# Squares and scaling of the first projection moved into the second one, and a second queue for the first input block

## The chip, the cores and the metric

The kernel runs on one core of a Trainium2 chip. The metric is the time of one execution on the device in microseconds (us). A core has engines with a queue of instructions each, which run beside one another and wait for each other by semaphores: TensorE (PE; its weight loads are PEld in the profile), VectorE (DVE), ScalarE (ACT), GpSimd (POOL) and SyncE (SP), which here only issues transfers.

## The reference

Two layers on x, 256 tokens by 2048 columns, in float32: an even one (retention and compressed, selected and windowed attention) and an odd one (convolution and dilated attention). Each normalizes its input and multiplies it by one wide weight matrix. The part around the change, cut:

```python
def rms_norm(x, gain):
    y = x * lax.rsqrt(jnp.mean(x * x, axis=-1, keepdims=True) + NORM_EPS)
    return y * gain
...
def compress(t, pos_emb, w1, w2):          # t: (batch, head, token, 128)
    idx = np.arange(n_cmp)[:, None] * CMP_STRIDE + np.arange(CMP_LEN)[None, :]
    blk = (t[:, :, idx] + pos_emb).reshape(B, G, n_cmp, CMP_LEN * d)
    return jax.nn.gelu(blk @ w1) @ w2
...
h = rms_norm(x, norm_g) @ w_in
rq, rk, rv, rz, nq, kc, vc, ks, vs, kw, vw, ng, nz = split_cols(h, EVEN_SPLITS)
kcmp = rms_norm(compress(heads(kc, G), pos_k, k_w1, k_w2), k_g[0])
vcmp = compress(heads(vc, G), pos_v, v_w1, v_w2)
```

Since the sum over a token's 2048 squares gives one factor per token, the kernel multiplies by the gain ahead of the matmul and by the token's factor `rstd` behind it.

## The kernel before

The kernel multiplies in slices of 512 weight columns, "projections". `project` goes through 2048 rows in four chunks of 512 rows (1 MB each, tile `raw`, three buffers). Of each chunk ACT makes the rounded part `wh` (L103) and DVE the rest `wl` (L104), in halves, and of the input block `xT` (four k-tiles of 128 rows by 256 tokens, held transposed) ACT makes `xh` (L185) and DVE `xl` (L186), both times the gain `evn`. PE adds up three products, wh by xh, wl by xh and wh by xl (L139 to L141): 24 matmuls of 512 columns a chunk, 96 a projection, into two PSUM banks `mm` for the two halves of the tokens. There are three such banks, so the next projection's first half can start in the third, and its second half needs the one that the first eviction of the projection before has emptied. Evictions are done by ACT.

The first projection makes `hkv` (keys and values for the compression), the second and the third `hs` (keys and values for the two attentions). In the first one ACT also squares each block of `xT` (L195), DVE sums the squares over k-tiles (L196) and over blocks (L201), PE over partitions with a column of ones (L204), and DVE and POOL make `rstd` from it (L210, L212), which the evictions of `hkv` and of every later projection take (L253). `hkv` is then transposed to `tT` (L274, L304), overlapping windows of it plus a position term are `blk` (L313), split in parts by ACT (L319) and DVE (L320) into `bhl` ahead of the compression's matmuls `cmph` (L340), which run between those of the third projection. `hs` is normed by head (square L260, sum `kn0ss` L262, POOL L168 and L169, product L265) and then transposed by PE.

Far later a row `rrow`, `rstd` along the free axis (`token_row`, L222 to L226), is made for the rotary tables in `pb` (L580, L581) and other projections.

Instructions are put in order by a scheduler of the framework with its own model of times; `tc.high_priority` puts an instruction ahead. The order on each engine is then fixed. All transfers go through SP's queue in the order that it gives them.

## Time and profile before

| | |
|---|---|
| time, median of 3 runs | 966.43 us (966.43, 966.43, 968.01) |
| profiled execution, its own time | 967.98 us |
| its span | 966.2 us |
| busy: PE, DVE, ACT, POOL | 950.3 (98%), 649.0 (67%), 521.1 (54%), 146.1 (15%) us |
| mean granted clock of PE | 0.998 |
| transfers | 171.53 MB, mean 178 GB/s |

The profiled execution's time is 1.8 us over its span; parts of a sum that is made from its rows belong to it and not to the median. A time behind "idle before" in a row is how long the engine stood still ahead of it, and behind the arrow stands what released it.

### The profile page before, as it was taken

The numbers are of one execution on the slowest core, as the hardware profiler recorded it, in microseconds if no ns is written. First come the engines' busy times: TensorE is split into PE (matmuls) and PEld (weight loads), VectorE is DVE, ScalarE is ACT, GpSimd is POOL, SyncE is SP. The second block draws the span as 40 slices with busy tenths as digits, with TensorE's granted clock in tenths as the row PEclk, the third lists the DMA queues.
The fourth block names the chain that finished last, engine by engine and source line by source line (L and its number), as shares of the span: only waits on it lengthen the run. The fifth ranks groups of instructions, "written<-read, shape, count | busy, mean of one in ns | idle before, by whom it ended". The sixth has DMA issues, their size and how long they took to land.

```text
span 966.2 us, 15609 instructions
## 1 busy us (share of the span) xinstructions
PE 950.3 (98%) x6401; PEld 873.3 (90%) x6401; DVE 649.0 (67%) x909; ACT 521.1 (54%) x727; POOL 146.1 (15%) x134
## 2 busy tenths in 40 slices
PE   8899999999999999999999999999999999999998
PEld 7688989899998998899999999888768889999998
DVE  7776556965654565655575579899889856545643
ACT  8366645755454444543364475555765556655532
POOL 0111010320211010000000294111771202000000
PEclk9999999999999999999999999999999999999999
DMA  9565753335445454555554445555445544433561
GB/s 314 205 214 181 234 208 132 128 135 175 163 163 185 165 174 175 184 181 197 180 176 174 175 165 185 192 200 175 173 137 214 181 171 171 169 125 144 197 211 73
DMA packets 31944, 171.53 MB, mean 178 GB/s; under 512 B 3328, under 2 KB 9600, under 8 KB 12800
## 3 DMA queue, kind: packets, MB, share of 16 engines
q1 hardware_dynamic: 31872, 170.53, 50.9%
q8 instruction: 50, 0.82, 0.3%
q14 instruction: 22, 0.18, 0.1%
HBM read 168.42 MB, written 2.10 MB: 176 GB/s over the span
## 4 chain that ended last, share of the span: by engine, by line
PE 88%; POOL 4%; ACT 3%; DVE 3%; issue 1%; DMA 0%; SPq 0%; POOLq 0%; ACTq 0%
PE mm L134 14%; PE mm L133 14%; PE mm L135 14%; PE mm L140 12%; PE mm L141 12%; PE mm L139 12%; POOL acc L737 3%; ACT wh L103 1%; PE tr L274 1%; DVE wl L104 1%; PE dpo L864 1%; PE dsc L844 1%; PE cmph L340 1%; DMA raw<-in_ew 0%; PE tr L529 0%
## 5 line engine op out<-in xcount | busy, mean ns | idle before, releaser
L104 DVE TENSOR_TENSOR wl<-raw,wh 128x1024 fp32r<-128x1024 f32 (+2 forms) x326 | 392.8, 1208 | 247.1 <-ACT wh L103 244.8
L103 ACT CAST wh<-raw 128x1024 fp32r<-128x1024 f32 (+2 forms) x326 | 328.8, 1012 | 338.9 <-PE mm L135 177.8
L134 PE MATMUL mm<-xh,wl 128*128 128x256 f32 x1280 | 362.3, 284 | 0.9 <-DVE wl L104 0.9
L133 PE MATMUL mm<-xh,wh 128*128 128x256 f32 x1280 | 360.6, 285 | 2.1 <-ACT wh L103 1.8
L135 PE MATMUL mm<-xl,wh 128*128 128x256 f32 x1280 | 360.4, 284 | 0.0
L134 PEld LDWEIGHTS mm<-xh,wl 128*128 128x128 f32 x1280 | 245.4, 192 | 1.8 <-DVE wl L104 1.5
L133 PEld LDWEIGHTS mm<-xh,wh 128*128 128x128 f32 x1280 | 243.6, 192 | 2.9 <-ACT wh L103 2.3
L135 PEld LDWEIGHTS mm<-xl,wh 128*128 128x128 f32 x1280 | 244.7, 192 | 0.1
L140 PE MATMUL mm<-wl,xh 128*128 128x512 f32 (+1 forms) x608 | 234.5, 387 | 6.1 <-DVE wl L104 6.0
L141 PE MATMUL mm<-wh,xl 128*128 128x512 f32 (+1 forms) x608 | 231.1, 381 | 0.0
L139 PE MATMUL mm<-wh,xh 128*128 128x512 f32 (+1 forms) x608 | 215.3, 384 | 1.4 <-ACT xh L185 0.8
L140 PEld LDWEIGHTS mm<-wl,xh 128*128 128x128 f32 x608 | 115.2, 190 | 31.5 <-DVE wl L104 10.6
L139 PEld LDWEIGHTS mm<-wh,xh 128*128 128x128 f32 x608 | 113.8, 189 | 23.3 <-ACT xh L185 1.1
L141 PEld LDWEIGHTS mm<-wh,xl 128*128 128x128 f32 x608 | 115.0, 189 | 20.7
L727 DVE SCALAR_TENSOR_TENSOR cps<-apad,pb,cps 128x256 f32<-128x256 f32 x180 | 87.5, 486 | 3.5
L737 POOL TENSOR_TENSOR acc<-acc,tap 128x256 f32<-128x256 f32 x60 | 60.1, 1001 | 14.0 <-ACT acc L733 8.4
L736 ACT ACTIVATE tap<-apad,pb 128x256 f32<-128x256 f32 x60 | 28.4, 503 | 16.9 <-POOL acc L737 14.0
L212 POOL TENSOR_TENSOR rstd<-rstd2m,mhalf 128x2 f32<-128x2 f32 x1 | 0.7, 695 | 162.3 <-DVE rstd2m L210 162.3
L593 POOL TENSOR_TENSOR rot<-rot,pb 128x512 f32<-128x512 f32 x8 | 11.1, 1402 | 79.7 <-ACT rot L591 79.6
L517 ACT ACTIVATE p<-p,nm 128x128 f32<-128x128 f32 (+1 forms) x32 | 14.2, 446 | 10.7 <-DVE nm L513 10.6
L196 DVE TENSOR_REDUCE sqs<-sqb 128x256 f32<-128x1024 f32 x8 | 16.0, 2004 | 0.3 <-ACT sqb L195 0.3
L686 DVE TENSOR_TENSOR xT<-mm,xT 128x512 f32<-128x512 f32 (+1 forms) x18 | 11.1, 630 | 5.1 <-PE mm L135 5.1
(272 smaller groups left out, 658.7 us busy)
## 6 DMA issues: line engine op xcount, KB each, us to landing
raw<-in_ow SPq DMA_DIRECT2D x64, 1024.0 KB, 4.8
raw<-in_ew SPq DMA_DIRECT2D x53, 1024.0 KB, 4.9
raw<-in_ewo SPq DMA_DIRECT2D x16, 1024.0 KB, 4.8
raw<-in_owo SPq DMA_DIRECT2D x12, 1024.0 KB, 4.9
raw<-in_ewn SPq DMA_DIRECT2D x8, 536.0 KB, 4.0
raw<-in_ew SPq DMA_DIRECT2D x12, 256.0 KB, 4.7
raw<-in_w1k SPq DMA_DIRECT2D x2, 1024.0 KB, 5.6
raw<-in_w1v SPq DMA_DIRECT2D x2, 1024.0 KB, 4.8
```

The source lines that it names most:

```text
L103: nc.scalar.copy(wh[:, k, :n], r)
L104: nc.vector.tensor_sub(wl[:, k, :n], r, wh[:, k, :n].bitcast(F32))
L133: nc.tensor.matmul(o, wh[:, k, cs], xh[:, kk, :], start=first and j == 0, stop=False, **kw)
L134: nc.tensor.matmul(o, wl[:, k, cs], xh[:, kk, :], start=False, stop=False, **kw)
L135: nc.tensor.matmul(o, wh[:, k, cs], xl[:, kk, :], start=False, stop=last, **kw)
L139: nc.tensor.matmul(o, xh[:, kk, ts], wh[:, k, :n], start=first, stop=False)
L140: nc.tensor.matmul(o, xh[:, kk, ts], wl[:, k, :n], start=False, stop=False)
L141: nc.tensor.matmul(o, xl[:, kk, ts], wh[:, k, :n], start=False, stop=last)
L196: nc.vector.reduce_sum(sqs[0][:, b, :], sq.rearrange("p k s -> p s k"), axis=AX.X)
L727: nc.vector.scalar_tensor_tensor(p, src[:, k:k + S], w[:, k:k + 1], p, op0=ALU.mult, op1=ALU.add)
L736: nc.scalar.activation(tap, src[:, k:k + S], AF.Copy, scale=w[:, k:k + 1])
L737: nc.gpsimd.tensor_add(dst, dst, tap)
```

## The change

The warm-up of PE gets 40 matmuls in place of 36. The first block of `xT` and the gains are loaded by ScalarE's queue and the weights alone by SP's at first. The first k-tile's `xh` is made by DVE. The squares leave the first projection: x is loaded a second time, by tokens (`xtok`, four pieces of 128 tokens by 1024 columns), and ACT squares and sums a piece in one instruction, after the first chunk of the second projection; `rstd` and `rrow` are made from that. The evictions of `hkv` are plain copies, and its transpose is scaled by `rrow`. The windows are made after the third chunk of the second projection in the program's text. The second layer's sum of squares is made by additions.

```diff
-WARM = 36
+WARM = 40
...
-            nc.scalar.activation(xh[:, k, :], x, AF.Copy, scale=g)
+            if first and k == 0:
+                nc.vector.tensor_scalar(xh[:, k, :], x, g, None, op0=ALU.mult)
+            else:
+                nc.scalar.activation(xh[:, k, :], x, AF.Copy, scale=g)
...
         nc.scalar.activation(sq, xT[:, 4 * b:4 * b + 4, :], AF.Square)
-        nc.vector.reduce_sum(sqs[0][:, b, :], sq.rearrange("p k s -> p s k"), axis=AX.X)
+        nc.vector.tensor_add(sq[:, 0:2, :], sq[:, 0:2, :], sq[:, 2:4, :])
+        if b == 0:
+            nc.vector.tensor_add(sqs[0], sq[:, 0, :], sq[:, 1, :])
+        else:
+            nc.vector.tensor_add(sq[:, 0, :], sq[:, 0, :], sq[:, 1, :])
+            nc.vector.tensor_add(sqs[0], sqs[0], sq[:, 0, :])
...
+    with tc.high_priority(offset=4 * HPO):
+        nc.scalar.dma_start(xT[:, 0, :], a["xT"][:, 0, :])
+        nc.scalar.dma_start(evn, a["ev_norm"])
+        nc.scalar.dma_start(xT[:, 1:4, :], a["xT"][:, 1:4, :])
...
-    def first_block(c):
-        load_block(c)
-        if c == 3:
-            for b in range(4):
-                square_block(b)
-            rstd.append(token_rstd(token_squares(sqs[0]), "rstd1"))
-
-    project(ew[0], 512, lhs, evac_to(hkv), lazy=first_block, cut=load_rest)
+    project(ew[0], 512, lhs, lambda t, p: nc.scalar.copy(hkv[:, t, :], p), lazy=load_block, cut=load_rest)
...
+    def times_row(dst, p, row):
+
+        nc.vector.tensor_tensor(dst, p.rearrange("p (k s) -> p k s", k=2),
+                                row.unsqueeze(1).to_broadcast([128, 2, S]), op=ALU.mult)
...
+    def windows():
+        tT = hp.tile([128, 4, S], F32, name="tT", tag="h")
+        for i in range(2):
+            pt = transpose4([hkv[:, t, (2 * i + g) * 128:(2 * i + g + 1) * 128] for g in range(2) for t in range(2)])
+            times_row(tT[:, 2 * i:2 * i + 2, :], pt, rrow)
...
+    def token_half(t):
+
+        for i in range(2):
+            sq = sp.tile([128, 1024], F32, name="sq", tag="sq")
+            nc.scalar.activation(sq, xtok[2 * t + i], AF.Square, accum_out=ssx[:, 2 * t + i:2 * t + i + 1])
+
+    def first_rstd():
+        tot = st.tile([128, 16], F32, name="xtot", tag="ss")
+        v = ssx[:, :4].rearrange("p (t i) -> p t i", t=2)
+        nc.vector.tensor_add(tot[:, :2], v[:, :, 0], v[:, :, 1])
+        rstd.append(token_rstd(tot[:, :2], "rstd1"))
+        token_row(rstd[0], "rrow", rrow)
+
+    for i in range(4):
+        x = hp.tile([128, 1024], F32, name=f"xtok{i}", tag="h")
+        nc.sync.dma_start(x, a["xtok"][:, i, :])
+        xtok.append(x)
+
+    squares = {0: [lambda: token_half(0), lambda: token_half(1), first_rstd], 2: [windows]}
     for br in range(2):
         h = htile(f"hs{br}")
         project(ew[1 + br], 512, lhs, evac_to(h),
-                extra={k: [compress(k // 2, k % 2)] for k in range(4)} if br else None)
+                extra={k: [compress(k // 2, k % 2)] for k in range(4)} if br else squares)
...
-    rrow = token_row(rstd[0], "rrow")
```

The order of instructions shows the change at three places. First DVE's queue at the end of the first projection, before; `L104` makes `wl`, `L186` makes `xl`, and the reduces sum the squares.

```order
-L104 TENSOR_TENSOR wl<-raw,wh 128x512
-L186 SCALAR_TENSOR_TENSOR xl<-xT,evn,xh 128x256
-L196 TENSOR_REDUCE sqs<-sqb 128x256
-L104 TENSOR_TENSOR wl<-raw,wh 128x512
-L186 SCALAR_TENSOR_TENSOR xl<-xT,evn,xh 128x256 x4
-L196 TENSOR_REDUCE sqs<-sqb 128x256
-L104 TENSOR_TENSOR wl<-raw,wh 128x1024 x2
-L201 TENSOR_REDUCE sq<-sqs 128x256
-L104 TENSOR_TENSOR wl<-raw,wh 128x1024 x2
-L210 TENSOR_SCALAR rstd1m<-tr 128x2
```

And DVE's queue there now, up to the end of the second projection: the reduces are gone, nine `wl` stand in a row (the last two of the first projection, and seven of the second), and `rstd` and the diagonal for `rrow` (`L228`) follow.

```order
+L189 SCALAR_TENSOR_TENSOR xl<-xT,evn,xh 128x256 x4
+L104 TENSOR_TENSOR wl<-raw,wh 128x1024 x9
+L443 TENSOR_TENSOR xtot<-xss 128x2
+L216 TENSOR_SCALAR rstd1m<-xtot 128x2
+L104 TENSOR_TENSOR wl<-raw,wh 128x1024
+L228 TENSOR_SCALAR sq<-pa,rstd_419 128x128 x2
+L104 TENSOR_TENSOR wl<-raw,wh 128x1024 x3
+L309 TENSOR_TENSOR tT<-tr,rrow 128x512
+L329 TENSOR_TENSOR blk_508<-tT,pa 128x32x15 x2
```

What moved: the sums left the place, and `tT` and the windows stand behind thirteen `wl`, four of which follow `rstd1m` and the diagonal.

Second, ACT's queue at the end of the second projection, before: the `bhl` casts are spread between the weight casts of this projection, and its two evictions `hs` follow weight casts.

```order
-L103 CAST wh<-raw 128x1024 x3
-L319 CAST bhl_389<-blk_386 128x16x30
-L319 CAST bhl_393<-blk_386 128x16x30
-L103 CAST wh<-raw 128x1024
-L319 CAST bhl_400<-blk_397 128x16x30
-L319 CAST bhl_404<-blk_397 128x16x30
-L103 CAST wh<-raw 128x1024 x3
-L253 ACTIVATE hs_415<-mm_416,rstd_329 128x512
-L253 ACTIVATE hs_415<-mm_417,rstd_329 128x512
```

And now (`L335` is the `bhl` cast, `L266` the eviction, `L273` its square):

```order
+L103 CAST wh<-raw 128x1024 x4
+L233 COPY rrow<-tr 128x256
+L335 CAST bhl_511<-blk_508 128x16x30
+L335 CAST bhl_515<-blk_508 128x16x30
+L266 ACTIVATE hs_370<-mm_371,rstd_419 128x512
+L266 ACTIVATE hs_370<-mm_372,rstd_419 128x512
+L273 ACTIVATE sq<-hs_370 128x512
+L426 CAST vh<-hs_370 128x512
+L335 CAST bhl_522<-blk_519 128x16x30
+L335 CAST bhl_526<-blk_519 128x16x30
```

What moved: the `rrow` copy and two `bhl` casts now stand between the weight casts and the two evictions of `hs`.

Third, DVE's queue behind the first windows, now (`L336` is the second part of `bhl`, `L275` the sum of squares by head, `L278` the scaling of `hs`):

```order
+L309 TENSOR_TENSOR tT<-tr,rrow 128x512
+L329 TENSOR_TENSOR blk_519<-tT,pa 128x32x15
+L336 TENSOR_TENSOR bhl_511<-blk_508,bhl_511 128x16x30
+L329 TENSOR_TENSOR blk_519<-tT,pa 128x32x15
+L336 TENSOR_TENSOR bhl_515<-blk_508,bhl_515 128x16x30
+L275 TENSOR_REDUCE kn0ss<-sq 128x4
+L427 TENSOR_TENSOR vl<-hs_370,vh 128x512
+L336 TENSOR_TENSOR bhl_522<-blk_519,bhl_522 128x16x30
+L336 TENSOR_TENSOR bhl_526<-blk_519,bhl_526 128x16x30
+L278 TENSOR_TENSOR hs_370<-hs_370,kn0rs 128x2x256
+L104 TENSOR_TENSOR wl<-raw,wh 128x1024 x3
```

What moved: in the order of before the windows and their parts stand among the `wl` of the second projection, and `kn0ss` and the scaling of `hs` each have a `wl` close by; now the sum `kn0ss` stands behind the windows, and the next `wl` behind the scaling of `hs`.

## Rows read from the trace of the kernel before

**Rows 1.** The page: busy us, share of the span, instructions of PE.

```profile
PE 950.3 (98%) x6401; PEld 873.3 (90%) x6401; DVE 649.0 (67%) x909; ACT 521.1 (54%) x727; POOL 146.1 (15%) x134
```

**Rows 2.** PE's timeline, 0 to 37: start us, duration, instruction, [idle before, releaser].

```profile
0.97 4.02 PE L162 MATMUL cold<-heat 128*128 128x128 bf16 x36 [0.97 <-DVE heat L159]
5.83 1.22 PE L139 MATMUL mm<-wh,xh 128*128 128x512 f32 x2 [0.84 <-ACT xh L185]
...
9.61 0.39 PE L141 MATMUL mm<-wh,xl 128*128 128x512 f32 x1
...
29.24 0.50 PE L140 MATMUL mm<-wl,xh 128*128 128x512 f32 x1 [2.86 <-DVE wl L104]
...
33.69 0.39 PE L140 MATMUL mm<-wl,xh 128*128 128x512 f32 x1
...
35.97 0.50 PE L204 MATMUL tr<-ones,sq 128*128 128x1 f32 x4
36.33 0.49 PE L139 MATMUL mm<-wh,xh 128*128 128x512 f32 x1
```

**Rows 3.** Windows: busy of PE, PEld, DVE, ACT, POOL; clock, DMA share, GB/s.

```profile
30.00:31.00 1.00, 1.00 (x4) 0.81 (x3) 1.00 (x2) 0.00 (x0) 0.00 (x0) 0.50 0.02 8
```

**Rows 4.** Lines, 5 to 36.3 us, DVE: busy, mean ns; idle before, releaser.

```profile
L104 DVE TENSOR_TENSOR wl<-raw,wh 128x512 fp32r<-128x512 f32 x12 | 8.4, 702 | 5.0 <-ACT wh L103 5.0
L196 DVE TENSOR_REDUCE sqs<-sqb 128x256 f32<-128x1024 f32 x4 | 8.0, 2006 | 0.3 <-ACT sqb L195 0.3
...
L186 DVE SCALAR_TENSOR_TENSOR xl<-xT,evn,xh 128x256 fp32r<-128x256 f32 x16 | 7.5, 494 | 0.2 <-ACT xh L185 0.2
```

**Rows 5.** Windows of the first projection, columns as in the group of windows above.

```profile
0.00:36.30 36.30, 30.72 (x136) 24.29 (x137) 28.21 (x38) 22.64 (x39) 0.76 (x9) 0.95 0.82 288
12.00:32.00 20.00, 16.23 (x64) 12.11 (x63) 20.00 (x28) 13.55 (x23) 0.00 (x0) 0.94 0.91 326
```

**Rows 6.** Timeline, first 5 us: SP's queue, and ACT's first cast.

```profile
0.72 0.39 SPq L234 DMA_DIRECT2D evn<-in_ev_norm  x1
1.17 0.42 SPq L92 DMA_DIRECT2D raw<-in_ew  x1
...
4.75 0.62 ACT L103 CAST wh<-raw 128x512 fp32r<-128x512 f32 x1 [2.52 <-DMA raw<-in_ew]
```

**Rows 7.** Timeline, 43 to 51 us, DVE and ACT: windows of the compression.

```profile
43.46 1.28 DVE L304 COPY tT<-tr 128x512 f32<-128x512 f32 x2
44.66 1.22 DVE L104 TENSOR_TENSOR wl<-raw,wh 128x1024 fp32r<-128x1024 f32 x1
45.79 3.76 DVE L313 TENSOR_TENSOR blk<-tT,pa 128x480 f32<-128x480 f32 x4
...
49.75 1.08 ACT L319 CAST bhl<-blk 128x480 fp32r<-128x480 f32 x2
```

**Rows 8.** Timeline, 58 to 66 us, ACT, DVE, PE: second projection ends.

```profile
58.24 0.69 ACT L253 ACTIVATE hs<-mm,rstd 128x512 f32<-128x512 f32 x1 [0.53 <-PE mm L141]
...
59.96 1.04 ACT L103 CAST wh<-raw 128x1024 fp32r<-128x1024 f32 x1
...
62.18 0.68 DVE L262 TENSOR_REDUCE kn0ss<-sq 128x4 f32<-128x512 f32 x1
...
65.54 0.69 DVE L265 TENSOR_TENSOR hs<-hs,kn0rs 128x512 f32<-128x512 f32 x1 [0.91 <-POOL kn0rs L169]
...
64.62 0.22 PE L340 MATMUL cmph<-wh,bhl 128*64 128x128 f32 x1
...
65.58 0.22 PE L340 MATMUL cmph<-wh,bhl 128*64 128x128 f32 x1
```

**Rows 9.** Timeline of PE, 174 to 180 us: rows with the longest waits.

```profile
174.71 0.38 PE L133 MATMUL mm<-xh,wh 128*128 128x256 f32 x1 [0.54 <-ACT wh L103]
...
176.10 0.47 PE L500 MATMUL sc<-kh,qh 128*128 128x512 f32 x1 [0.68 <-DVE nm L510]
```

**Rows 10.** Timeline of DVE at 559 us, beside POOL's accumulation.

```profile
559.50 1.67 DVE L104 TENSOR_TENSOR wl<-raw,wh 128x1024 fp32r<-128x1024 f32 x1
```

More of the change, by code (lines that the diff above doesn't have):

```diff
@@ L177, in hybrid_kernel, with norm_block @@
     sqs = [None]
-    def norm_block(b, gain):
+    def norm_block(b, gain, first=False):
         xh = xtp.tile([128, 4, S], F32R, name="xh", tag="xh")
@@ L216, in hybrid_kernel, with token_row @@
     nc.gpsimd.memset(ones128, 1.0)
-    def token_row(r, name):
+    def token_row(r, name, row=None):
         dg = sp.tile([128, 1024], F32, name="sq", tag="sq")
@@ L224, in token_row @@
         nc.tensor.matmul(pt[:, :S], ones128, dg[:, :S], start=True, stop=True)
-        row = const.tile([128, S], F32, name=name)
+        if row is None:
+            row = const.tile([128, S], F32, name=name)
         nc.scalar.copy(row, pt[:, :S])
@@ L233, in load_block @@
             if b == 0:
[L234 removed]
+                return
             if b < 3:
@@ L241, in load_rest @@
     def load_rest(b, k):
-        if k < 3:
+        if k == 3:
+            lhs.append(norm_block(b, evn, first=b == 0))
+        elif b:
             nc.sync.dma_start(xT[:, 4 * b + k + 1, :], a["xT"][:, 4 * b + k + 1, :])
-        else:
-            lhs.append(norm_block(b, evn))
     def htile(name):
@@ L300, in hybrid_kernel @@
     kng = small["kng"]
-    tT = hp.tile([128, 4, S], F32, name="tT", tag="h")
-    for i in range(2):
-        pt = transpose4([hkv[:, t, (2 * i + g) * 128:(2 * i + g + 1) * 128] for g in range(2) for t in range(2)])
-        nc.vector.tensor_copy(tT[:, 2 * i:2 * i + 2, :].rearrange("p a b -> p (a b)"), pt)
+    def times_row(dst, p, row):
+        nc.vector.tensor_tensor(dst, p.rearrange("p (k s) -> p k s", k=2),
+                                row.unsqueeze(1).to_broadcast([128, 2, S]), op=ALU.mult)
@@ L306, in hybrid_kernel @@
+    rrow = const.tile([128, S], F32, name="rrow")
     blks = []
-    for i, pos in enumerate((posk, posv)):
-        blk = hp.tile([128, CMP_LEN, 2 * N_CMP], F32, name=f"blk{i}", tag="h")
-        for g in range(2):
-            src = tT[:, 2 * i + g, :]
-            win = bass.AP(tensor=src.tensor, offset=src.offset,
-                          ap=[list(src.ap[0]), [1, CMP_LEN], [CMP_STRIDE, N_CMP]])
-            nc.vector.tensor_tensor(blk[:, :, g * N_CMP:(g + 1) * N_CMP], win,
-                                    pos.unsqueeze(2).to_broadcast([128, CMP_LEN, N_CMP]), op=ALU.add)
-        for c in range(2):
-            b = hp.tile([128, 16, 64], F32R, name=f"bhl{i}{c}", tag="h")
-            nc.gpsimd.memset(b.bitcast(F32), 0.0)
-            v = blk[:, 16 * c:16 * c + 16, :]
-            nc.scalar.copy(b[:, :, 0:30], v)
-            nc.vector.tensor_sub(b[:, :, 32:62], v, b[:, :, 0:30].bitcast(F32))
-            blks.append(b)
+    def windows():
[3 more added lines that the diff above has]
+            times_row(tT[:, 2 * i:2 * i + 2, :], pt, rrow)
+        for i, pos in enumerate((posk, posv)):
+            blk = hp.tile([128, CMP_LEN, 2 * N_CMP], F32, name=f"blk{i}", tag="h")
+            for g in range(2):
+                src = tT[:, 2 * i + g, :]
+                win = bass.AP(tensor=src.tensor, offset=src.offset,
+                              ap=[list(src.ap[0]), [1, CMP_LEN], [CMP_STRIDE, N_CMP]])
+                nc.vector.tensor_tensor(blk[:, :, g * N_CMP:(g + 1) * N_CMP], win,
+                                        pos.unsqueeze(2).to_broadcast([128, CMP_LEN, N_CMP]), op=ALU.add)
+            for c in range(2):
+                b = hp.tile([128, 16, 64], F32R, name=f"bhl{i}{c}", tag="h")
+                nc.gpsimd.memset(b.bitcast(F32), 0.0)
+                v = blk[:, 16 * c:16 * c + 16, :]
+                nc.scalar.copy(b[:, :, 0:30], v)
+                nc.vector.tensor_sub(b[:, :, 32:62], v, b[:, :, 0:30].bitcast(F32))
+                blks.append(b)
@@ L414, in split @@
             nc.vector.scalar_tensor_tensor(lo, src, g, hi.bitcast(F32), op0=ALU.mult, op1=ALU.subtract)
+    xtok, ssx = [], st.tile([128, 16], F32, name="xss", tag="ss")
+    def token_half(t):
[13 more added lines that the diff above has]
+    squares = {0: [lambda: token_half(0), lambda: token_half(1), first_rstd], 2: [windows]}
     for br in range(2):
@@ L942 @@
     arr["xT"] = A(x.T.reshape(KT, 128, S).transpose(1, 0, 2))
+    arr["xtok"] = A(x.reshape(2, 128, 2, 1024).transpose(1, 0, 2, 3)).reshape(128, 4, 1024)
     arr["ev_norm"] = A(i["ev_norm"][0].reshape(KT, 128).T)
```

10 lines of the change are left out of this document (2 added, 8 removed).

## The prediction

> **What bounds the kernel now.** I read the page first: TensorE is busy 98% of the span, so only time in which it waits, or runs slowly, can be won [rows 1]. Then the timeline of PE from the start to the end of the first projection. The warm-up takes 4.02 us for 36 matmuls, or 0.112 each; the first real matmul starts at 5.83 and the first one of the second projection at 36.33, so the stretch takes 30.5 us [rows 2]. It has 96 matmuls of 512 columns. Where nothing disturbs them they follow each other at 0.228 us (ten from 33.69 to 35.97) [rows 2], so 96 need 21.9. The other 8.6 us are four things, all in the same rows: waits for DVE's `wl`, the longest of them 2.86; nine matmuls from 5.83 to 9.61 at 0.42 instead of 0.228 (1.7 lost); twelve from 29.24 to 33.69 at 0.37 (1.7 lost); and 0.36 for the four small `tr<-ones,sq` between 35.97 and 36.33. For the twelve the windows show why: the granted clock was 0.50 from 30 to 31 us, the 1.2 GHz level, after the wait of 2.86 [rows 3]. The lines of this stretch and the window from 12 to 32 name the engine behind the waits: DVE was busy all 20.00 of 20.00 us [rows 5]. Per weight chunk it had four `wl` of 0.70, four `xl` of 0.49 and one `reduce_sum` of 2.01 [rows 4], 6.8 us, where PE needs 24 x 0.228 = 5.5.
>
> **Part 1: the squares leave the first projection.** DVE is left with 4 x 0.70 + 4 x 0.49 = 4.8 us a chunk, below PE's 5.5, so the waits for `wl` behind the first chunk go, and the slow clock behind the 2.86 with them. The `tr<-ones,sq` matmuls go as well.
>
> **Part 2: the start.** With 40 warm-up matmuls the warm-up ends at 0.97 + 40 x 0.112 = 5.44. The first weight piece was issued at 1.17, behind the gains at 0.72, and its cast began 3.58 later [rows 6]; issued first, at 0.72, its cast would begin at 4.3 and end at 4.9, and the first `xh`, now DVE's and independent of ACT, is ready by then too. So the first matmul starts at 5.44. The three other k-tiles of the block come in one transfer on ScalarE's queue beside four weight pieces. About 1.0 MB must land before the second k-tile can start; at the 326 GB/s of the first projection [rows 5] that is 3.2 us behind a first landing near 3.7, so about 6.9, and one `xh` and one `xl` of 0.5 each behind it give 8.0. PE has six matmuls until 6.8, so 1.2 us are lost: an estimate, with 0.7 and 2.0 as bounds (data at 7.5 or at 8.8). The second projection then begins at 5.44 + 21.9 + 1.2 = 28.5, and 36.33 - 28.5 = **7.8 us are won** (7.0 to 8.3).
>
> **Part 3: squares by tokens.** Four loads of 0.5 MB, four ACT squares of 128x1024 and small DVE and POOL steps are added in the second projection. The nearest row for such a square is the cast of the same size, 1.04 [rows 8]; four come to 4.2 us. ACT then has eight casts and these in 21.9 us, and they stand behind casts that PE wants only later. I cost them at nothing; the cover would be gone if the loads landed late (rival 4).
>
> **Part 4: what now stands at the end of the second projection.** Here I expect a new loss. The transposes of `hkv`, their scaling by `rrow`, the windows `blk` and the casts `bhl` were spread over the second projection; now they come at its end, and in ScalarE's queue two `bhl` casts stand ahead of the `hs` evictions. PE's `mm_589` needs a third bank that only the first of these evictions frees. Count from T1, the end of the last matmul of the second projection. ACT's last `wh` cast waits for buffers that this matmul frees; 0.2 for its end and 1.04 for the cast [rows 8] give 1.24, the `rrow` copy (256 columns, 0.3 estimated from the `bhl` casts of 480 at 0.54) 1.52. DVE's `wl` (1.13 from its start to the next one's) ends at 2.4, `tT` 0.64 later at 3.04, two `blk` of 0.94 at 4.92. ACT's two `bhl` casts at 0.54 [rows 7] end at 6.0; the first `hs` eviction (0.69 [rows 8]) starts at 6.15 and ends at 6.85. PE meanwhile does the `rrow` matmul (0.35, an estimate from the 0.36 of the four small ones), four transposes (0.45), the twelve of `mm_588` (2.74) and four transposes (0.45): it stands before `mm_589` at 4.0. It waits **2.9 us**. Next is late what follows the evictions: the second ends at 7.44 and its square at 8.0. DVE has, from 4.92, another `tT`, two `blk` and two `bhl` differences ahead of `kn0ss` (0.64 + 1.88 + 1.2, the differences estimated by the `tT` row), so `kn0ss` (0.68) ends at 9.3. From its end, 62.18 + 0.68 = 62.86, to the start of `hs<-hs,kn0rs` at 65.54 POOL takes 2.7, and that instruction 0.69 [rows 8]: `hs` is ready at 12.6. PE has done `mm_589` (6.85 + 2.74) and sixteen `cmph` (some 1.1 [rows 8]) at 10.8, and waits another **1.8**. DVE's next `wl` stand behind this `hs`, which costs about 0.25 three times, **0.7**. Sum 5.4 us lost. Bounds: nothing, if the eviction isn't held; 7.1, if the clock falls once more.
>
> **Part 5: the `rrow` copy leaves its old place.** Around it, at 174 to 180 us, PE waits 0.54 and 0.68 [rows 9], 1.2 in all, the first of them for a cast that stands beside the `rrow` copy in ACT's queue. The order there changes only in part; I take two thirds as won, **0.8** (0 to 1.2, for nothing and all). In the second layer, the reduce of squares is replaced by additions; PE doesn't wait there in the trace of before, so this is worth nothing.
>
> **Sum.** The profiled execution of before took 967.98 us. 967.98 - 7.8 + 5.4 - 0.8 = **964.8**, 0.17% under the median of the runs shown (966.43), to which a difference of 0.2%, about what the measurement can tell from no change, is 1.9 us. The 1.55 us between the profiled execution and the median is about one stretch of slow clock (1.7), so the changed kernel may also come out that much lower.
>
> **Rivals.** 1, the evictions are not held: PE gets its bank in time, because ACT and DVE are ahead of PE by more than I count, or the wait is as short as that of the evictions in before, which stand right behind a cast [rows 8]. For it: DVE is no longer behind in the second projection. Against: the `bhl` casts need `tT`, and that needs `rrow`, in a fixed order. Without the 5.4 and with a rest of 0.7: 960.1. 2, the clock falls: the wait of 2.86 was followed by about 4 us of clock 0.50 [rows 2, 3], which cost 1.7. After the new wait of 2.9 the same is likely, but the chain to `hs` hides it, since PE would stand before the transposes anyway; only a second fall after the wait of 1.8 costs another 1.7: 966.5. The Trainium skill ("TensorE: Matmul & The Clock Gate", section "What's actually happening") says that the throttled state is the default and activity releases it; the rows agree with it for a wait of 2.86 and don't show one of 1.8. 3, POOL delays DVE: the two multiplications of `pb` by `rrow` now run at T1 + 1.5 to 3.0 (0.72 each in the old place), beside `wl`. A `wl` of this shape took 1.67 beside POOL's additions at 559 us [rows 10] against about 1.15. Two such delays of 0.4 move the whole chain by 0.8: 965.6. The Trainium skill ("SBUF — State Buffer", section "Who interferes with whom") has it as a rule that DVE and GpSimd share a port pair under an exclusive lock; the 1.67 agrees, and by it this rival would be the forecast. 4, the other side: the transfers. By the time that the last weight chunk of the second projection is there, 12.5 MB have come: four chunks (4.2), x by columns (2.1), the packs (1.0), half of x by tokens (1.0) and four chunks more (4.2). PE wants that chunk at 28.5 + 3 x 5.5 = 45, and its first half must be cast and subtracted before, so it must land by 42.5. Behind a start at 1.2 this needs 303 GB/s on average; 288 were moved in the first 36.3 us of before, 326 from 12 to 32, both with pauses for buffers [rows 5]. At 288 PE waits 2.1, at 278 3.7, and from there on the kernel is slower than before by over 0.2%: 968.5. Against: the pauses for buffers should be shorter.
>
> **How the numbers follow.** Forecast, 963.3 to 966.3 by the bounds of parts 2 and 5: 0.48. Rival 1 (960.1): 0.20. Rival 2: 0.12. Rival 3: 0.10. Rival 4: 0.10, of which 0.08 above 968.4. The range 959.8 to 967.6 takes in rival 1's time and leaves out its lower half and most of rival 4, together under 2 in 10. Below 964.5 (faster): rival 1 and somewhat over half of the forecast, whose lower part is widened by the 1.55, 0.47. Above 968.4: 0.08. Within: 0.45.
>
> **What would show it.** PE's first 512-column matmul near 5.4, no wait over 0.3 for `wl` behind 10 us, the second projection beginning near 28.5; then a wait of 2 to 3 us for the `hs` eviction some 4 us behind the end of the second projection, and one of 1 to 2 at the transposes of `hs`. No such waits: rival 1. A clock of 0.50 behind the second: rival 2. `wl` over 1.4 near 52: rival 3. Waits for `raw` or `xtok` before 50: rival 4. I am wrong if the loss at the end of the second projection is under 2 or over 8 us.

## The result, and the profile after

The changed kernel takes 972.58 us (median of 10 runs, 970.06 to 975.39) against 968.00 for the kernel before on the same chip; the ratio is 1.0054, 95% interval 1.0036 to 1.0071. The forecast was 964.8, with 959.8 to 967.6 as range. It is slower by about 5 us where a gain of 3 was forecast. One of the ten runs of the kernel before took 2540.94 us; the median gives it no weight. The profiled execution of the changed kernel took 975.39, the slowest of its ten.

PE's share stays at 98%, and its busy time hardly moves; what came on top is waiting. From the page, the line of the engines:

```profile
PE 951.1 (98%) x6401; PEld 874.5 (90%) x6401; DVE 638.8 (66%) x912; ACT 521.4 (54%) x730; POOL 147.4 (15%) x134
```

PE's timeline from the start to the end of the first projection, as in [rows 2]:

```profile
0.97 4.19 PE L162 MATMUL cold<-heat 128*128 128x128 bf16 x40 [0.97 <-DVE heat L159]
7.04 0.70 PE L139 MATMUL mm<-wh,xh 128*128 128x512 f32 x2 [1.88 <-ACT wh L103]
8.07 0.74 PE L140 MATMUL mm<-wl,xh 128*128 128x512 f32 x1 [0.33 <-DVE wl L104]
...
9.04 0.63 PE L140 MATMUL mm<-wl,xh 128*128 128x512 f32 x1
9.47 0.63 PE L141 MATMUL mm<-wh,xl 128*128 128x512 f32 x1
...
27.39 0.73 PE L139 MATMUL mm<-wh,xh 128*128 128x512 f32 x2 [1.56 <-ACT wh L103]
28.65 0.80 PE L140 MATMUL mm<-wl,xh 128*128 128x512 f32 x1 [0.53 <-DVE wl L104]
...
30.10 0.63 PE L140 MATMUL mm<-wl,xh 128*128 128x512 f32 x1
30.52 0.63 PE L141 MATMUL mm<-wh,xl 128*128 128x512 f32 x1
...
35.38 0.39 PE L139 MATMUL mm<-wh,xh 128*128 128x512 f32 x1
```

The first matmul starts at 7.04, not at 5.44, and the second projection at 35.38, not at 28.5; before it was 36.33. The wait for `wl` of 2.86 that stood in [rows 2] is gone, as the forecast had it. In its place PE waits 1.56 for the first half of the last chunk's weights at 27.39, and there are two stretches in which the matmuls follow each other at 0.43 instead of 0.227 (9.04 to 9.47, and 30.10 to 30.52). From 7.04 and the 21.9 that 96 matmuls need the end would be 28.9; the other 6.4 are the waits of 0.33, 1.56 and 0.53, which make 2.4, and 4.0 that go in the main to the two slow stretches. The windows (columns as in [rows 3]) show the granted clock at 0.50, its lower level of 1.2 GHz, in both, and at 1.00 behind the wait of 3.02 at 64.41, which is shown further down:

```profile
9.00:10.00 1.00, 1.00 (x4) 0.77 (x3) 1.00 (x4) 1.00 (x4) 0.00 (x0) 0.50 0.92 246
30.00:31.00 1.00, 1.00 (x4) 0.72 (x4) 1.00 (x1) 0.00 (x0) 0.00 (x0) 0.50 0.88 172
64.00:66.00 2.00, 1.59 (x7) 1.35 (x8) 2.00 (x4) 1.97 (x4) 0.52 (x1) 1.00 0.00 0
```

What ended these waits is in the timelines of DVE, SP's queue, and ACT with its queue:

```profile
6.54 0.35 DVE L186 TENSOR_SCALAR xh<-xT,evn 128x256 fp32r<-128x256 f32 x1 [5.63 <-DMA evn<-in_ev_norm]
...
16.33 0.83 SPq L95 DMA_DIRECT2D raw<-in_ew  x2
...
1.15 0.46 ACTq L241 DMA_DIRECT2D evn<-in_ev_norm  x1
...
26.30 2.00 ACT L103 CAST wh<-raw 128x1024 fp32r<-128x1024 f32 x2 [0.89 <-DMA raw<-in_ew]
```

The first `xh` waited for the gains (`evn`), which were issued at 1.15 and landed at 6.5; it and ACT's second `wh`, which PE's row names, both ended at 6.9. The last chunk of the first projection was issued at 16.33 and the first one of the second projection right with it (`x2`); ACT could begin the cast of the last chunk at 26.30. In the kernel before, the last chunk went out at 15.25 and the next one at 18.76, when its buffer had come free, and ACT cast the last one at 22.61, without a wait for its landing:

```profile
22.61 1.98 ACT L103 CAST wh<-raw 128x1024 fp32r<-128x1024 f32 x2
```

At the end of the second projection (PE, ACT, DVE and POOL), as in [rows 8]:

```profile
57.13 0.59 PE L230 MATMUL tr<-sq,ones 128*128 128x256 f32 x2
...
64.41 0.50 PE L139 MATMUL mm<-wh,xh 128*128 128x512 f32 x1 [3.02 <-ACT hs L266]
...
70.62 0.63 PE L462 MATMUL tr<-pa,hs 128*128 128x128 f32 x4 [2.20 <-DVE hs L278]
...
62.68 1.09 ACT L335 CAST bhl<-blk 128x480 fp32r<-128x480 f32 x2 [4.03 <-DVE blk L329]
63.68 1.26 ACT L266 ACTIVATE hs<-mm,rstd 128x512 f32<-128x512 f32 x2
...
60.28 2.32 DVE L329 TENSOR_TENSOR blk<-tT,pa 128x480 f32<-128x480 f32 x2
...
69.78 0.69 DVE L278 TENSOR_TENSOR hs<-hs,kn0rs 128x512 f32<-128x512 f32 x1 [1.19 <-POOL kn0rs L169]
...
58.73 1.51 POOL L616 TENSOR_TENSOR pb<-pb,rrow 128x256 f32<-128x256 f32 x1 [7.73 <-ACT rrow L233]
60.20 0.74 POOL L617 TENSOR_TENSOR pb<-pb,rrow 128x256 f32<-128x256 f32 x1
```

This is the chain of part 4, with its waits to within 0.4 us and its times to within 0.9: counted from the `rrow` matmul at 57.13, the end of the projection, `mm` gets its bank at 7.28 (forecast 6.85) after a wait of 3.02 (2.9), and the transposes of `hs` start at 13.5 (12.6) after a wait of 2.20 (1.8).

At 180 us, PE as in [rows 9], with DVE and POOL:

```profile
180.10 0.38 PE L133 MATMUL mm<-xh,wh 128*128 128x256 f32 x1 [0.76 <-ACT wh L103]
182.80 0.55 PE L133 MATMUL mm<-xh,wh 128*128 128x256 f32 x1 [2.31 <-DVE rT L628]
...
174.88 3.47 DVE L525 CAST pst<-pch 32x256 fp32r<-32x256 f32 x8
178.36 3.35 DVE L525 CAST pst<-pcl 32x256 fp32r<-32x256 f32 x8
...
181.97 0.69 DVE L628 TENSOR_TENSOR rT<-mm,pb 128x512 f32<-128x512 f32 x1
...
176.61 1.30 POOL L629 TENSOR_TENSOR rot<-rot,pb 128x512 f32<-128x512 f32 x1 [24.00 <-ACT rot L627]
179.06 1.32 POOL L629 TENSOR_TENSOR rot<-rot,pb 128x512 f32<-128x512 f32 x1 [1.15 <-ACT rot L627]
```

Here a gain of 0.8 was forecast. PE waits 0.76 and 2.31, the latter for the bank that DVE's `rT<-mm,pb` frees; DVE comes to it at 181.97, behind sixteen casts `pst` that take 3.47 + 3.35 = 6.8 us, and two products `rot` on POOL lie beside them. These last are new here: before, POOL waited for `rrow` until 175.01, when the casts were done. The matmuls behind it follow each other at 0.21 until 185.49 and at 0.12 from there.

### The profile page after: what moved, and what is told of

The parts are those of the page before. It is cut to its first block, busy times and chain, and to the rows that moved or that the text cites. A ratio compares the mean times of both kernels' runs of the same rounds, so it can differ in the third digit from the quotient of the medians.

```text
span 973.6 us, 15618 instructions
## 1 busy us (share of the span) xinstructions
PE 951.1 (98%) x6401; PEld 874.5 (90%) x6401; DVE 638.8 (66%) x912; ACT 521.4 (54%) x730; POOL 147.4 (15%) x134
## 4 chain that ended last, share of the span: by engine, by line
PE 86%; POOL 4%; DVE 3%; DMA 2%; ACT 2%; issue 1%; ACTq 0%; POOLq 0%; SPq 0%
PE mm L134 14%; PE mm L133 14%; PE mm L135 14%; PE mm L140 12%; PE mm L141 12%; PE mm L139 12%; POOL acc L768 4%; DMA raw<-in_ew 2%; ACT wh L103 1%; PE tr L287 1%; DVE wl L104 1%; PE dpo L895 1%; PE dsc L875 1%; PE cmph L356 1%; DVE pst L525 1%
## 5 line engine op out<-in xcount | busy, mean ns | idle before, releaser
L104 DVE TENSOR_TENSOR wl<-raw,wh 128x1024 fp32r<-128x1024 f32 (+2 forms) x326 | 393.2, 1209 | 254.7 <-ACT wh L103 252.3
L139 PEld LDWEIGHTS mm<-wh,xh 128*128 128x128 f32 x608 | 113.4, 189 | 29.4 <-ACT wh L103 4.8
L767 ACT ACTIVATE tap<-apad,pb 128x256 f32<-128x256 f32 x60 | 28.5, 505 | 16.9 <-POOL acc L768 14.0
L630 POOL TENSOR_TENSOR rT<-rT,rot 128x512 f32<-128x512 f32 x8 | 14.0, 1767 | 2.6 <-DVE rT L628 2.6
```

The source lines that it names most:

```text
L104: nc.vector.tensor_sub(wl[:, k, :n], r, wh[:, k, :n].bitcast(F32))
L139: nc.tensor.matmul(o, xh[:, kk, ts], wh[:, k, :n], start=first, stop=False)
L767: nc.scalar.activation(tap, src[:, k:k + S], AF.Copy, scale=w[:, k:k + 1])
```

## The experiments

The first compression's second product (`cmpk`) and the first scores of the retention (`rsc`) are marks that every kernel has. From them and from the start of the second projection (where it can be read, by PE's timeline or, 0.2 ahead, by the second eviction of `hkv`) each profiled execution splits in three; from `rsc` to the end of the span it is 697.9 us before and 698.2 after. Times of the profiled execution in us, medians and ratios over all runs. The kernels ran in several groups, each on one chip together with new runs of before, and each ratio is to these; two medians of different groups can differ by about 0.5 for that alone.

| kernel | 2nd projection starts | from there to `cmpk` | `cmpk` to `rsc` | median | ratio to before, interval |
|---|---|---|---|---|---|
| before | 36.3 | 44.8 | 187.2 | 967.5 to 968.0 | |
| changed | 35.4 | 51.1 | 188.9 | 972.58 | 1.0054 (1.0036 to 1.0071) |
| e1_start_only | 35.0 | 44.8 | 187.2 | 968.28 | 1.0004 (0.9996 to 1.0013) |
| e2_old_start | 35.2 | 51.1 | 189.1 | 974.48 | 1.0065 (1.0053 to 1.0077) |
| e3_warm56 | 31.9 | 51.1 | 189.2 | 971.82 | 1.0044 (1.0030 to 1.0058) |
| e4_packs_late | 31.4 | 51.2 | 187.7 | 971.17 | 1.0038 (1.0026 to 1.0050) |
| e5_rrow_early | 35.9 | 45.2 | 190.2 | 970.77 | 1.0028 (1.0016 to 1.0040) |
| e6_pieces | 31.6 | 51.2 | 189.1 | 971.55 | 1.0037 (1.0025 to 1.0049) |
| e7_prio | 31.8 | 48.0 | 189.1 | 970.15 | 1.0033 (1.0021 to 1.0046) |
| e8_rrow_twice | 35.1 | 50.7 | 187.3 | 969.75 | 1.0028 (1.0018 to 1.0037) |
| e9_all | 29.4 | 49.8 | 187.2 | 967.53 | 0.9999 (0.9989 to 1.0008) |
| e10_adds | 31.1 | 44.8 | 187.2 | 963.12 | 0.9955 (0.9943 to 0.9967) |
| e11_bank | 31.5 | 47.3 | 189.1 | 968.36 | 1.0012 (1.0001 to 1.0023) |
| e12_best | 30.9 | 47.1 | 187.2 | 965.15 | 0.9971 (0.9960 to 0.9982) |

In e1 and e10 one matmul of the second projection runs ahead of the four small `tr<-ones,sq`; their 35.0 and 31.1 are counted as if it stood behind them, as it does in the kernel before.

**The start alone, and the start taken back.** e1 is the kernel before with the new start only, e2 the changed kernel with the old one.

```diff
+        nc.scalar.dma_start(xT[:, 0, :], a["xT"][:, 0, :])
+        nc.scalar.dma_start(evn, a["ev_norm"])
+        nc.scalar.dma_start(xT[:, 1:4, :], a["xT"][:, 1:4, :])
...
-                nc.sync.dma_start(evn, a["ev_norm"])
```

> The kernel before with only the new start (40 warm-up matmuls, first input block and gains by ScalarE's queue, weights first on SP's, first xh by DVE). Theory A, the transfers of the start share one supply: four weight pieces and the block go out within 2 us, the gains land late (6.5 us in the changed kernel's trace), the first matmul starts near 7.0 instead of 5.8, PE has stood still for 1.9 and the clock falls; about 1 to 2 us slower than before: 968 to 970. Rival B, the start is good and the loss comes from later parts: first matmul at or before 5.8, 965.5 to 967.5.

> The changed kernel with the start of before (36 warm-up matmuls, all on SP's queue, xh by ACT); the squares stay out of the first projection. Theory A: first matmul near 5.8, no fall of the clock at 8.5, the last chunk's weights land some 2 to 4 us sooner than 26.3, the second projection begins near 31 instead of 35.4; 967 to 970. Rival B (the start isn't what costs; the transfers are late because of what is issued behind the third chunk): the second projection still begins at 34 or later, 971 to 975.

e1 is no different from before (968.28): its first matmul came at 5.70, as rival B had it, and its time lies in theory A's range, so neither held whole; the new start by itself neither costs nor wins. The Trainium skill ("DMA: Bandwidth & Descriptors", section "Issuing engines are not separate DMA queues") says that transfers issued by several engines run on the same DMA engines, and only the time to issue is saved; e1, no different from before with a second queue, agrees. e2 is no faster than the changed kernel (974.48; the intervals overlap). Its PE timeline:

```profile
5.77 0.73 PE L139 MATMUL mm<-wh,xh 128*128 128x512 f32 x2 [0.78 <-ACT xh L185]
...
26.34 1.22 PE L139 MATMUL mm<-wh,xh 128*128 128x512 f32 x2 [2.81 <-ACT wh L103]
...
35.20 0.39 PE L139 MATMUL mm<-wh,xh 128*128 128x512 f32 x1
```

The old start gives the first matmul at 5.77, and still PE waits 2.81 for the last chunk's weights and begins the second projection at 35.2. So rival B was right on the start: the long first projection is not its doing.

**A longer warm-up.**

```diff
-WARM = 40
+WARM = 56
```

> The changed kernel with 56 warm-up matmuls in place of 40, which end near 6.9, about when the first operands are ready. Theory A: the ten matmuls at the low clock behind 8.5 run at the full one, but the last chunk's weights land when they did (near 26.3), so PE only waits longer there, and the second projection still begins near 35 us: 971 to 975, within 0.8 of the changed kernel. Rival C (PE and its clock limit the first projection): it begins 1.8 earlier, 968.5 to 972.5, about 1.8 under the changed kernel.

Theory A's time came out, but neither picture did. The matmuls behind the start kept the full clock, and the second projection began at 31.9; but the last chunk also landed sooner, ACT casting it at 24.41 instead of 26.30, which more warm-up matmuls don't explain. The median is 0.8 under the changed kernel, inside the intervals. The changed kernel's own runs spread over 5 us; its profiled execution, the slowest, had a late landing and two falls of the clock in the first projection, which the faster runs need not have.

**Constants later, and the last chunk in pieces.** e4 is the changed kernel with the packs of constants `pm` and `pb` loaded behind `hkv`; e6 loads the last chunk and its block of `xT` in pieces, as the other chunks are.

```diff
         t = const.tile([128, sum(n for _, n in PACKS[name])], ...)
+        if name != "pa":
+            nc.gpsimd.tensor_copy(t[:, 0:1], hkv[:, 0, 0:1])
         nc.sync.dma_start(t, a[name])
```

> The changed kernel with 0.74 MB of constants (tiles pm and pb) loaded only after the first projection's evictions instead of behind its last weight chunk. The traces of the runs so far have the transfer engines busy for 0.9 to 1.0 of the time from 6 to 28 us in every kernel, and the same 8 MB moved by 26. Theory A, transfers in flight share the engines: with less in flight the last chunk of the first projection lands up to 1.8 us earlier than 26.3, its wait of about 1.6 shrinks, and the second projection begins up to 1.8 (with the fall of the clock 3.5) earlier; 969 to 971.5. Rival F, they are served in order of issue: nothing moves, 971.5 to 973.5.

```diff
-            parts = prep(src[c], n, cut=(lambda k: cut(c, k)) if cut and i < 3 else None)
+            parts = prep(src[c], n, cut=(lambda k: cut(c, k)) if cut and i < 4 else None)
...
-            if b < 3:
+            if b < 4:
```

> The changed kernel with the fourth weight chunk of the first projection and its input block loaded in four pieces each, as the first three are. Theory A, PE waits near 25.7 because the whole chunk of 1 MB must land, while the transfer engines are full: a first piece is there by 23, PE's wait of 1.6 and 0.5 at that chunk and the fall of the clock behind it go, the second projection begins near 31 to 32; 968.5 to 971. Rival G (the bytes themselves come too late, whatever the pieces): waits of the same sum, spread over the pieces, 972 to 974.

In e4 ACT cast the last chunk at 23.93, and in e6 PE had no wait over 0.3 at the last chunk, which speaks against rival G; the second projections began at 31.4 and 31.6. In e6 what is left is PE's own: the first matmul at 6.70, 21.9 for 96 matmuls, and 3.0 for the slow ones behind a fall of the clock at the start. The medians are 1.4 and 1.0 under the changed kernel, but the intervals overlap, and e3 and e7 began it nearly as early without either edit. That PE waits for the last chunk's landing in the changed kernel is shown by the rows; which of the transfers beside it makes it late is not.

**The chain at the end of the second projection.** e7 is the changed kernel with a higher priority for the second load, the squares, `rrow` and the windows; e11 puts the second projection into another pair of PSUM banks, so that the third one doesn't wait for its evictions.

```diff
-        nc.sync.dma_start(x, a["xtok"][:, i, :])
+        with tc.high_priority(offset=3 * HPO):
+            nc.sync.dma_start(x, a["xtok"][:, i, :])
...
-    squares = {0: [lambda: token_half(0), lambda: token_half(1), first_rstd], 2: [windows]}
+    def ahead(f):
+        def g():
+            with tc.high_priority(offset=HPO):
+                f()
+        return g
+
+    squares = {0: [ahead(lambda: token_half(0)), ahead(lambda: token_half(1)), ahead(first_rstd)], 2: [ahead(windows)]}
```

> The changed kernel with a higher priority for the second load of x, its squares, rstd, rrow and the windows: PE's matmul for rrow and the first transposes then stand 24 matmuls (5.4 us) earlier, ahead of the last chunk of the second projection. Theory H, the loss of about 6.4 us between the start of the second projection and the first compression is the chain rrow, windows, bhl, hs eviction, kn0ss, hs: most of it goes, waits of under 1 us in place of 3.0 and 2.2, 967 to 969. Rival I (the chain is set by ACT's and DVE's work as a whole and not by its start): waits fall by less than half, 970 to 973; or the second load, now ahead of the last two weight chunks, makes PE wait for raw.

```diff
+        if bank:
+            both = ps.tile([128, 1024], F32, name="mmsc", tag=bank)
+            acc = [both[:, t * 512:(t + 1) * 512] for t in range(2)]
...
-        project(ew[1 + br], 512, lhs, evac_to(h),
+        project(ew[1 + br], 512, lhs, evac_to(h), bank=None if br else "sc",
```

> The changed kernel with the second projection's sums in the two banks that only later stages use, so that PE needn't wait for the eviction of hs before the third projection. Theory J, the wait of 3.0 is one for a bank: the scheduler now puts 24 matmuls of the third projection ahead of the compression, the chain runs beside them, and the 6.4 us between the start of the second projection and the first compression's end shrink to 2 to 3: 967.5 to 969. Rival K, the chain itself sets it: the 3.0 only moves to the transposes of hs, 971 to 973.

Of the 6.3 us by which the stretch from the second projection to `cmpk` grew (44.8 to 51.1), the earlier start of the chain took 3.1 away and the free banks 3.8. In e7 the wait of 3.02 is gone and one of 1.89 at the transposes of `hs` is left; in e11, where PE has matmuls of the third projection in between, both are gone, and waits of 1.34 and 0.54 for `wl` stand there instead. PE's timeline at this place in e7:

```profile
63.83 0.63 PE L469 MATMUL tr<-pa,hs 128*128 128x128 f32 x4 [1.89 <-DVE hs L278]
```

And in e11:

```profile
62.81 0.27 PE L360 MATMUL cmph<-wl,bhl 128*64 128x128 f32 x1 [1.34 <-DVE wl L104]
```

So theory J came out (2.5 of the 6.3 are left), and theory H for about half (3.2 are left, and 970.15 lies in rival I's range): the chain is the cause, as forecast, and it can be started earlier or covered. The medians fell by 2.4 and 4.2.

A fall of the clock costs nothing at this place. In e2, e3, e4 and e6 it fell behind the same wait of 3.0, and the wait at the transposes of `hs` shrank from 2.20 to 0.6 or to none, while the stretch to `cmpk` stayed at 51.1 to 51.2. PE's timeline and a window (columns as in [rows 3]) of e4:

```profile
66.67 0.63 PE L464 MATMUL tr<-pa,hs 128*128 128x128 f32 x4 [0.60 <-DVE hs L280]
```

```profile
63.00:64.00 1.00, 1.00 (x4) 0.81 (x3) 1.00 (x3) 1.00 (x2) 1.00 (x1) 0.50 0.00 0
```

**The row `rrow` at 180 us.** e5 is the kernel before with the row made early; e8 the changed kernel that makes it again at the old place. The edit of e5, and that of e8:

```diff
     kng = small["kng"]
+    rrow = token_row(rstd[0], "rrow")
...
-    rrow = token_row(rstd[0], "rrow")
     cosR = small["cosT"]
```

```diff
+    rrow = token_row(rstd[0], "rrow2")
     cosR = small["cosT"]
```

> The kernel before with the row rrow made in the second projection instead of far later, nothing else changed; DVE's order from there on is then that of the changed kernel. Theory D, the reordering around 180 us costs: waits for the cast and for rT of about 0.8 and 2.3 and a fall of the clock behind them, in place of 1.2 of waits: 968.5 to 971, about 1.5 to 2.5 above before. Rival E (the waits there come of the later start of everything, or of other parts): no wait over 1 us at 170 to 190, time within 0.8 of before.

> The changed kernel which in addition makes the row rrow a second time at its old place, for the rotary tables and all later uses. Theory D, what costs at 180 us is the order that came of taking rrow away there: waits of 0.8 and 2.3 and the fall of the clock go back to about 1.2 of waits, 969 to 971 (the changed kernel less 2 to 3). Rival E: they stay, 972 to 974.

That the early row is the cause held in both directions. PE's timeline at this place in e5:

```profile
174.76 0.38 PE L133 MATMUL mm<-xh,wh 128*128 128x256 f32 x1 [0.78 <-ACT wh L103]
177.44 0.55 PE L133 MATMUL mm<-xh,wh 128*128 128x256 f32 x1 [2.30 <-DVE rT L592]
```

And those of PE, DVE and POOL in e8:

```profile
179.46 0.38 PE L133 MATMUL mm<-xh,wh 128*128 128x256 f32 x1 [0.55 <-ACT wh L103]
...
180.87 0.47 PE L537 MATMUL sc<-kh,qh 128*128 128x512 f32 x1 [0.70 <-DVE nm L547]
...
174.65 2.37 DVE L525 CAST pst<-pch 32x256 fp32r<-32x256 f32 x8
...
177.34 2.38 DVE L525 CAST pst<-pcl 32x256 fp32r<-32x256 f32 x8
...
179.76 0.73 POOL L617 TENSOR_TENSOR pb<-pb,rrow 128x256 f32<-128x256 f32 x1 [27.78 <-ACT rrow L233]
```

e5 has the two waits of the changed kernel though nothing else differs in its edit from before, and costs 2.8 us (ratio 1.0028); e8 has those of [rows 9] again. The rows of DVE and POOL show how. In e8 POOL is held by the late `rrow` until 179.76 and the two groups of eight casts take 2.37 and 2.38, as they do in the kernel before. In the changed kernel, in e4 and in e5 POOL has its `pb` long done and multiplies `rot` as soon as ACT has copied it; the same casts take 3.47 and 3.35 there, 2.1 us more in all, and `rT`, for whose bank PE waits 2.30 to 2.32, stands behind them. A kernel that keeps the early row and moves only POOL's products out of the way was not run, so that 2.1 of these 2.3 come from the meeting is worked out and not tried. PE's order differs as well: before, six `sc` matmuls and eleven of the projection stand between the wait for the cast (174.71) and the one for `rT` (179.32); in the changed kernel the one for `rT` comes next, with nothing of these in between. No run separates this from the longer casts. Where the waits are 0.76 and 2.31, the stretch from `cmpk` to `rsc` takes 187.7 (no fall of the clock, e4) to 190.2 (a long one, e5), against 187.2: the waits alone cost 0.5, and the slow clock behind them the rest.

**Only the sums by additions.** The kernel before, with the squares where they were:

```diff
-        nc.vector.reduce_sum(sqs[0][:, b, :], sq.rearrange("p k s -> p s k"), axis=AX.X)
+        nc.vector.tensor_add(sq[:, 0:2, :], sq[:, 0:2, :], sq[:, 2:4, :])
+        if b == 0:
+            nc.vector.tensor_add(sqs[0], sq[:, 0, :], sq[:, 1, :])
+        else:
+            nc.vector.tensor_add(sq[:, 0, :], sq[:, 0, :], sq[:, 1, :])
+            nc.vector.tensor_add(sqs[0], sqs[0], sq[:, 0, :])
...
-        nc.vector.reduce_sum(tot[:, :S], xs.rearrange("p b s -> p s b"), axis=AX.X)
```

> The kernel before with only the sum of squares made by additions (128x512, 128x256, 128x256 for a block) in place of the reduces; the squares stay in the first projection. If DVE's queue sets the first projection of before, some 0.6 us a block and 1.95 at the end are taken off it, the wait of 2.86 for wl shrinks to under 1 and the clock doesn't fall behind it: 964 to 966. Rival: the transfers, which are full until 28 us, take over at once, 966.5 to 968.

It is the fastest of all, 963.12, 4.4 us under before and a little under the range. DVE's lines in the first projection (columns as in [rows 4]):

```profile
L196 DVE TENSOR_TENSOR sqb<-sqb 128x512 f32<-128x512 f32 x4 | 2.8, 688 | 0.3 <-ACT sqb L195 0.3
L201 DVE TENSOR_TENSOR sqs<-sqs,sqb 128x256 f32<-128x256 f32 x3 | 1.3, 421 | 0.0
L200 DVE TENSOR_TENSOR sqb<-sqb 128x256 f32<-128x256 f32 x3 | 1.3, 418 | 0.0
```

Its window from 12 to 28 us (columns as in [rows 3]):

```profile
12.00:28.00 16.00, 15.41 (x67) 12.13 (x66) 15.78 (x31) 13.44 (x23) 0.00 (x0) 1.00 1.02 377
```

And PE's timeline at the last chunk:

```profile
25.62 0.50 PE L140 MATMUL mm<-wl,xh 128*128 128x512 f32 x1 [0.53 <-DVE wl L104]
```

A block's sum costs 0.69 + 0.42 + 0.42 = 1.5 in place of 2.01 [rows 4], and the reduce of 1.95 over blocks at the end is gone. The one wait for `wl` left is 0.53, the clock holds behind it, and the second projection begins at 31.1. That is as early as in e3, e4, e7 and e11 (31.4 to 31.9), which have no squares there at all. DVE is still busy 15.78 of 16.00 us in this window and the transfer engines are at a share of 1.02. e3, e4, e7 and e11 begin no earlier, but not because of DVE: there PE starts at 6.4 to 6.6 and waits 0.5 to 1.6 for the last chunk. e9, below, begins earlier.

**All edits of the changed kernel together.** e9 has e6, e7 and e8 in one, e12 has e11 too.

> The changed kernel with three of the edits above together: four pieces for the fourth chunk, the higher priority for rstd, rrow and windows, and rrow made a second time at its old place. If the three causes are separate (transfers at the start, chain at the end of the second projection, order at 180 us), their gains add: second projection at 31.4 (4.9 sooner than before), 3.2 lost until the first compression, nothing at 180 us: 968.0 - 4.9 + 3.2 = 966.3, range 965 to 967.5. Rival: the gains overlap, since a wait that is taken away early comes back at the next one, 968 to 970.

> All of it: the changed kernel with four pieces for the fourth chunk, the higher priority, rrow twice, and the two other banks for the second projection. If the four causes are what the runs so far say: second projection at 31.4, about 0.7 lost behind it for the matmul with rrow, nothing at 180: 968.0 - 4.9 + 0.7 = 963.8, range 962.5 to 965.5, faster than before. If a cause is missing: 966 to 968.

e9 wins back what the changed kernel lost (967.53 after 972.58), just above the range of its forecast. In its profile the second projection begins at 29.4, the earliest of all. PE's timeline and a window:

```profile
6.32 0.70 PE L139 MATMUL mm<-wh,xh 128*128 128x512 f32 x2 [1.19 <-ACT wh L103]
...
29.41 0.39 PE L139 MATMUL mm<-wh,xh 128*128 128x512 f32 x1
```

```profile
12.00:28.00 16.00, 16.00 (x72) 13.27 (x71) 11.78 (x23) 11.59 (x22) 0.00 (x0) 1.00 0.99 354
```

With the last chunk in pieces PE doesn't wait for it, and the clock holds at the start: the 96 matmuls take 23.1, 1.2 over the undisturbed 21.9, although the transfer engines have a share of 0.99. So full transfer engines do not by themselves set the length of this projection. In e6 and e9 the next chunk is also issued later (19.76 and 20.35, for 16.33), and no run has the pieces without that.

Of the lead of 2.4 over e7 only 0.6 is left at `cmpk` (79.2 and 79.8), since the chain now starts late for another reason. PE, DVE and POOL in e9:

```profile
47.37 0.67 PE L230 MATMUL tr<-sq,ones 128*128 128x256 f32 x2 [1.47 <-DVE sq L228]
...
43.53 3.69 DVE L228 TENSOR_SCALAR sq<-pa,rstd 128x128 f32<-128x128 f32 x2 [0.89 <-POOL rstd L218]
...
43.45 3.63 POOL L333 MEMSET bhl<- 128x1024 f32 x4
```

The two DVE products that make the diagonal for `rrow` take 3.69 where they take 0.48 in the changed kernel and in e7. Beside them lie POOL's four memsets of `bhl`, which come right behind `rstd` here, and later, behind the two `pb` products, in those two. In e8 and e12 the memsets lie at the same place as in e9, and the products take 2.88 and 2.80.

The banks give 2.4 more (e12, 965.15, inside its range). e12 beats the kernel before by 0.3%, and is still 2.0 above e10. What is left in its profile is the first matmul at 6.68 with a fall of the clock behind it, a wait of 0.58 ahead of the `rrow` matmul, for these products, and two for `wl` of 0.34 and 0.70.

## Why the prediction was wrong, step by step

On the profiled executions the forecast missed by 10.6 us (975.39 for 964.8). The step that failed most is part 2's, the 7.8 won at the start (0.95 measured, 6.9 of the miss): it let 96 matmuls run on behind the start and put the landing of the last weight chunk at nothing. Then part 5's sign (2.5), part 4's size (0.9), and 0.3 in the rest. Falls of the clock are in these numbers; the median, 972.58, is missed by 7.8.

- **Part 1, right in its place and wrong in its size.** The waits for `wl` behind the first chunk went, but for 0.53. What I took for the limit behind DVE, PE's 21.9 us, was not the next one: it is the landing of the last chunk, 1 MB in one transfer. [Rows 5] had a sign of it, a transfer share of 0.91 from 12 to 32. I read that row only for a rate to use in rival 4, and placed the trouble in the second projection, where it didn't come. e2 shows the new limit most plainly: first matmul at 5.77, and at the last chunk 2.81 of waiting for it to land. e6 and e9, with this chunk in pieces, have no such wait, and in e9 PE's own work is the limit but for 1.2.
- **Part 2, mis-sized: 0.95 measured for 7.8, about 5 in the better executions, 6.9 in e9.** In e3, e4, e7 and e11 the second projection begins at 31.4 to 31.9. Of the 2.9 to 3.4 between that and 28.5 about 1.1 are the first matmul (6.54 in e4, for 5.44; it waited for the first `xh`, and so for the gains; why these landed late isn't shown) and 0.5 to 1.6 the waits at the last chunk; the rest, about 1, are slow matmuls and short waits in the first chunks. The other 3.5 to 4.0 of the profiled execution are the falls of the clock and a later landing, which come in part of the profiles.
- **Part 3, right.** No wait for the second load or its squares is in the rows, so rival 4 didn't come in its place.
- **Part 4, right, 5.4 forecast and 6.3 measured.** The waits were 3.02 and 2.20 for 2.9 and 1.8. What I left out is PE's own time for the `rrow` matmul, 0.43 (57.13 to 57.56), which I had put into the chain but not into the sum; about 0.6 more is in no row as a wait, nor are the three delays by `wl` that I put at 0.7. Rival 2's argument held, that the chain hides a fall of the clock behind the first wait (e2, e3, e4, e6). Rival 3's mechanism also came: POOL's first `pb` product took 1.51 where it had taken 0.72, and the two `blk` beside it and beside the memsets 2.32 where [rows 7] have 1.88 for two, the first of them 1.44. The Trainium skill ("SBUF — State Buffer", section "Who interferes with whom") says that DVE and GpSimd share a port pair under an exclusive lock; the rows agree with it, here and at 180 us.
- **Part 5, wrong in sign.** I took the waits at the old place of `rrow` as caused by its copy in ACT's queue, and asked only what is gained when it goes. The failing step is that I didn't ask what the late row had held back: it kept POOL still until DVE's casts were through (idle 27.78 ahead of its product in e8, as in the kernel before). With the row early, POOL's `rot` products meet these casts and lengthen them by 2.1, and 0.8 forecast as won became 1.7 lost in the changed kernel and 3.0 in e5; 0.5 of it without a fall of the clock (e4). It is the same meeting as in rival 3, priced by [rows 10], at a place where I had not looked for it.
- **The sum.** For the profiled executions: 0.95 won at the start, 6.3 lost behind it, 1.7 lost at 180, and 0.3 in the rest, 7.4 in all, which is 975.39 - 967.98. In the forecast's own sum the band 963.3 to 966.3 doesn't follow from the bounds of parts 2 and 5, which give 963.9 to 966.4. No rival named this outcome: rival 4 had transfers as its mechanism, but at the wrong chunk and with a chance of 0.1.

The clock is no cause by itself, but it makes a wait dearer at the start and at 180 us: it fell behind waits of 1.88, 1.56 and 2.31 in the changed kernel's profile and not behind the one of 3.02, nor behind the 2.20. In e6, behind a wait of 3.03 at the place of the 3.02, the window from 61 to 62 us has it at 0.50, and in e4 a wait of 2.32 at the place of the 2.31 left it whole. The Trainium skill ("TensorE: Matmul & The Clock Gate", section "What's actually happening") makes the throttled state the default that activity lifts; the falls agree with that; whether one comes behind a wait of this size the runs here don't settle.

What stays open is why ACT could begin the cast of the first projection's last chunk at 22.61 in the kernel before, at 23.25 in e10, between 23.9 and 24.4 in e4 and e3, and only at 26.30 in the changed kernel. There the next chunk is in flight with it, issued at 16.33 where before it went out at 18.76, because its buffer is free sooner. But in e3 the two went out together as well, at 16.31, and the last chunk was there 1.9 us sooner, so this is not the whole cause, and a kernel that holds back this chunk alone was not run.
